# Gather of the first expert right after its one-hot columns, with the expert sorting, one residual scale and the scatter rows placed after it

## Chip, cores and metric

One core of one Trainium2 chip runs the whole program as one launch. The metric is the device time of that core in microseconds (us). Several executions of a kernel are timed and their median is quoted; one more execution is recorded by the hardware profiler, and all rows below come from that one.

## Reference

Two layers run over 256 tokens of 1024 features. Each layer has a mixer with three kinds of attention heads, and then a channel mixer: dense in layer 0, and eight experts of which each token uses its best two in layer 1. Only the expert stage and the step before it matter here:

```python
logits = (t @ w_router).astype(jnp.float32)
top_v, top_i = lax.top_k(logits, TOP_K)
gates = jax.nn.softmax(top_v, axis=-1)
combine = jnp.sum(jax.nn.one_hot(top_i, N_EXPERTS, dtype=jnp.float32) * gates[..., None], axis=1)
for e in range(N_EXPERTS):
    out = out + combine[:, e:e + 1] * swiglu(t, w1[e], w3[e], w2[e])
...
x = layer_norm(DEEPNORM_ALPHA * x + (1.0 + g2) * y, ln2_g[l], ln2_b[l])
```

`swiglu` is `(silu(h @ w1) * (h @ w3)) @ w2` with 1024 x 3584 weights in float32. An expert's three matrices are 44 MB, and all eight are read from HBM.

## Kernel before

The program is one long function, `trunk`, written in the order in which each engine is to run: nothing reorders it. TensorE (PE), VectorE (DVE), ScalarE (ACT) and GpSimd (POOL) each take their own instructions in that order, and the queue SP issues the weight transfers. A transfer waits until the buffer it fills has been read. In the expert stage 16 weight buffers of 1 MB are in turn: five `raws`, three `raws2`, two that were lent by tiles no longer in use, and six made of a `whi` and a `wlo` half (`load_ahead`, L330 and L335).

**Routing** comes after the second layer's mixer. Logits are compared (`choose`), five small matmuls (L1454 to L1458) count who stands before each token, and L1459 writes `slot`, the place of a token in its expert's list. `one_hot(0)` (L1395) turns the first expert's slots into one-hot columns `oh`. Then DVE sorts the experts by how many tokens they have (L1463 to L1494). From that come `slot_at` and `gate_at`, the slots and gates in sorted order, `turn`, the numbers of the experts, which SP reads before it loads the second expert, and `flag`. Expert 0 always comes first and needs no sorting.

**The second residual scale** `grow[1, 1]` has two halves of 512 columns. Each is a bias addition on DVE (`held`, L579), a matmul that spreads a row over all partitions (`later`, L596), and an activation on ACT (L597). The second half is made after the sorting. From the finished scale six ACT copies make the `gain` tiles (L1515).

**Expert stage.** Places with 96 and with 64 columns of tokens alternate; place 0 has 96. For each place:

- `gather(e)` puts four steps in a list. `part(0)` and `part(1)` multiply the normalised tokens `xhat` by `oh` (16 fp32 matmuls of 96 columns in all, L1526), and each scales its half of `xe`, on ACT or, for the second half of place 0, on DVE (`affine`, L619 and L621). `back(0)` and `back(1)` make one-hot rows for the way back: DVE compares (L1534), PE turns (L1538), ACT copies to `ohT` (L1540). `tick()` runs one step of the list.
- Work goes by chunks c = 0 to 3 of the hidden width, here written place/chunk. `up` takes two weight blocks at a time, a group g, in four groups: eight matmuls for the first 64 columns (L1565) into two banks `h`, and eight for the other 32 (L1573) into two banks `hov` that are shared by all chunks and set to 0 once (L1509). After each group it calls `between`, and that calls `tick()`.
- `gated` applies Silu: ACT (L1584) and DVE (L1585) for `h`, then for each `hov` bank an ACT copy (L1591), a DVE addition (L1592) after which the bank is free, Silu on ACT (L1594) and a product on DVE (L1595). It is turned (L1604, in the next chunk's first `between`) and multiplied by `w2` (`down`, L1619 and L1625) after the next chunk's `up`.
- `scatter` multiplies the result by `gain`, adds it to the residual through `ohT`, again as steps.

Place 0 runs its four steps at once, with `tick(4)`, before its first `up`.

Of the kernel before, what the change touches and what calls it, by code (L numbers as in the profile page):

```python
# [9 lines left out]
FT = mybir.dt.float32  # L10
FR = mybir.dt.float32r
BF = mybir.dt.bfloat16
I32 = mybir.dt.int32
AF = mybir.ActivationFunctionType
OP = mybir.AluOpType
AX = mybir.AxisListType.X

S = 256
D = 1024
NB = S // 128  # L20
KD = D // 128
# [103 lines left out]
CAP, BASE = 96, 64  # L125
CAPS = (CAP, BASE) * (NE // 2)
# [4 lines left out]
def trunk(ctx: ExitStack, tc: tile.TileContext, a, out, manual=True):  # L131
    nc = tc.nc
    mm, tr = nc.tensor.matmul, nc.tensor.transpose
    vec, act, pool = nc.vector, nc.scalar, nc.gpsimd
# [3 lines left out]
    small = ctx.enter_context(tc.tile_pool(name="small", bufs=2))  # L138
# [4 lines left out]
    def bank():  # L143
        return psum.tile([128, 512], FT, name="bk", tag="bk")
# [6 lines left out]
    grow = {}  # L151
# [56 lines left out]
    for l in range(2):  # L208
# [28 lines left out]
        if l == 0:  # L237
            ada_weights(0, 11, 12)
            for t in range(12):
# [5 lines left out]
                if t in DENSE_ADA:  # L245
                    n = DENSE_ADA[t]
                    ada_weights(1, n, n + 1)
            ada_weights(1, 5, 6)
        else:
            ada_weights(1, 10, 12)  # L250
            for n in range(NE * 4 + 1):
                e, c = divmod(n, 4)
                if e < NE:
                    k = 8 * 256 // COLS[c]
# [4 lines left out]
                if n > 0:  # L259
                    e, c = divmod(n - 1, 4)  # L260
# [17 lines left out]
    def lend(tag):  # L278

        lent.add(tag)  # L280
        spare.append(tag)
# [109 lines left out]
    start = ExitStack()  # L391
# [33 lines left out]
    ident = cf[:, C_ID:C_ID + 128]  # L425
# [14 lines left out]
    ps = bank()  # L440
# [11 lines left out]
    ps = bank()  # L452
# [6 lines left out]
    ps = bank()  # L459
# [5 lines left out]
    steps = []  # L465
# [3 lines left out]
    def tick(n=1):  # L469
        if sums:  # L470
            sums.pop(0)()
        if aside:
            aside.pop(0)()
        while n > 0 and steps:
            step = steps.pop(0)
            n -= 1
            if step is not None:
                step()
# [18 lines left out]
    later = []  # L497
# [56 lines left out]
    held = []  # L554
# [60 lines left out]
    def affine(f, ps, k0, ac, bc, eng):  # L615
        for i in range(4):
            k = k0 + i
            if eng is act:
                act.activation(f[:, i], ps[:, i], AF.Identity, scale=ac[:, k:k + 1], bias=bc[:, k:k + 1])  # L619
            else:  # L620
                eng.tensor_scalar(f[:, i], ps[:, i], ac[:, k:k + 1], bc[:, k:k + 1], op0=OP.mult, op1=OP.add)  # L621
# [614 lines left out]
    ac = base.tile([128, 8], FT, name="acol", tag="acol", bufs=2)  # L1236
# [43 lines left out]
    for bits in (6, 8, 10, None):  # L1280
        if bits is None:
            c = float(np.float32(rest))
        else:
            e = 2.0 ** (bits - 1 - np.floor(np.log2(rest)))
# [81 lines left out]
    es = ExitStack()  # L1366
    moe = places = None
# [12 lines left out]
    oh, ohT = {}, {}  # L1380
# [6 lines left out]
    slot_at = moe.tile([128, NB, NE], FT)  # L1387
# [3 lines left out]
    def one_hot(e):  # L1391
        n = CAPS[e]
        oh[e] = moe.tile([128, NB, CAP], FT, name="oh", bufs=2)
        for b in range(NB):
            vec.tensor_scalar(oh[e][:, b, 0:n], iota[:, 0:n], (slot if e == 0 else slot_at)[:, b, e:e + 1], None,  # L1395
                              op0=OP.is_equal)

    with tc.tile_pool(name="route", bufs=1) as rt:
        lg = rt.tile([128, NB, NE], FT)
        sel = rt.tile([128, NB, NE], FT)  # L1400
# [27 lines left out]
        def choose(b):  # L1428
# [24 lines left out]
        ps = bank()  # L1453
# [5 lines left out]
        vec.scalar_tensor_tensor(slot, ps[:, 0:16].rearrange("p (b e) -> p b e", b=2), 1.0, sel,  # L1459
                                 op0=OP.add, op1=OP.mult)  # L1460
        one_hot(0)
        num = rt.tile([128, NE], FT)
        vec.tensor_copy(num, ps[:, 16:24])  # L1463
        rank = ranks(num)
# [28 lines left out]
        vec.tensor_scalar(most, most, 0.0, None, op0=OP.max)  # L1493
        vec.tensor_copy(flag, most)  # L1494

    held.pop(0)()
    later.pop(0)()
    gr2 = grow[1, 1]

    with es:
        ep = es.enter_context(tc.tile_pool(name="expert", bufs=1))

        hov = [bank() for _ in range(2)]
        yov = bank()
        for ps in (*hov, yov):
            vec.memset(ps, 0.0)  # L1509

        gain = [ep.tile([128, 512], FT, name=f"gain{i}") for i in range(2)]
        for g, n in zip(gain, (64, 32)):
            for q in range(0, 128, n):
                hf = q // n % 2
                act.activation(g[q:q + n], gr2[q:q + n, 512 * hf:512 * hf + 512], AF.Copy)  # L1515

        def gather(e):
            xe = ep.tile([128, KD, CAP], FT, name="xe", bufs=2)
            n = CAPS[e]

            def part(g):
                ps = bank()[:, 0:4 * n].rearrange("p (k t) -> p k t", k=4)
                for i in range(4):
                    k = 4 * g + i
                    for b in range(NB):
                        mm(ps[:, i], xhat[:, b, 128 * k:128 * k + 128], oh[e][:, b, 0:n], start=b == 0, stop=b == NB - 1)  # L1526
                affine(xe[:, 4 * g:4 * g + 4, 0:n], ps, 4 * g, ac, bc, vec if e == 0 and g == 1 else act)

            def back(v):

                f = small.tile([128, 4, 128], FT, name="aff")
                ps = bank()
                for b in range(NB):
                    vec.tensor_scalar(f[:, 2 * b:2 * b + 2], places[:, 2 * v:2 * v + 2], slot_at[:, b, e:e + 1], None,  # L1534
                                      op0=OP.is_equal)
                for b in range(NB):
                    for hf in range(2):
                        tr(ps[:, 256 * hf + 128 * b:256 * hf + 128 * b + 128], f[:, 2 * b + hf], ident)  # L1538
                ohT[e, v] = moe.tile([128, 2, S], FR, name="ohT", bufs=4)
                act.activation(ohT[e, v], ps.rearrange("p (h t) -> p h t", h=2), AF.Copy)  # L1540

            steps.extend([lambda: part(0), lambda: part(1), lambda: back(0)])
            if n > BASE:
                steps.append(lambda: back(1))
            return xe

        def used_up(raw):
            raw["left"] = 1
# [49 lines left out]
        def gated_turn(e, f, n):  # L1598
            gT = ep.tile([128, 8, CAP], FT, name="egT")
            t = CAPS[e]  # L1600
            for g in range(n // 4):
                ps = bank()
                for j in range(4):
                    tr(ps[:, t * j:t * j + t], f[0:t, 512 * g + 128 * j:512 * g + 128 * j + 128], ident[0:t, 0:t])  # L1604
                ps = ps[:, 0:4 * t].rearrange("p (j t) -> p j t", j=4)
                if g == 0:
                    act.activation(gT[:, 0:4, 0:t], ps, AF.Copy)  # L1607
                else:
                    vec.tensor_copy(gT[:, 4:8, 0:t], ps)  # L1609
            return gT  # L1610
# [70 lines left out]

        work = base.tile([128, 4, 4, 128], FR, name="work", tag="t2")
        order = [(e, c) for e in range(NE) for c in range(4)]
        xes = {0: gather(0)}
        tick(4)
        ys = {}
        fs = {}
        rows = None
# [1 line left out]
        for n in range(len(order) + 1):  # L1690
            if n < len(order):
                e, c = order[n]

                def between(g):

                    if n > 0 and g == 0:
                        fs[n - 1] = gated_turn(order[n - 1][0], fs[n - 1], COLS[order[n - 1][1]] // 128)
                    tick()

                h = up(e, c, xes[e], between)  # L1700
                fs[n] = gated(e, h)
                if e + 1 < NE:
                    if c == 0:
                        one_hot(e + 1)
                    if c == GATHER_AT:
                        xes[e + 1] = gather(e + 1)
                    if (e, c) == ROWS_AT:
                        returned("t3")
                        mid = spread_rows(1, 0)
                        steps.append(lambda: (residual(mid, xhat), aside.append(lambda: lend("t3"))))  # L1710
                    if (e, c) == LEND_TO:
                        lent.clear()
                        spare.clear()
                    if (e, c) == LAST_ROWS_AT:
                        returned("t3")
                        rows = spread_rows(1, 1)
            else:
                fs[n - 1] = gated_turn(NE - 1, fs[n - 1], 4)
            if n > 0:
                pe, pc = order[n - 1]  # L1720
                if pc == 0:
                    ys[pe] = bank()
                if n == len(order):
                    tick(20)
                down(pe, pc, fs.pop(n - 1), ys[pe])
                if pc == 3:
                    scatter(pe, ys.pop(pe))
# [5 lines left out]
    def more(first):  # L1733

        with tc.tile_pool(name="more", bufs=1) as xp:
            en = xp.tile([128, 1], FT)
            vec.memset(en, 1.0)
            with tc.For_i(0, NE, 1) as e:
# [16 lines left out]
                ps = bank()  # L1755
# [4 lines left out]
                for g in range(2):  # L1760
                    ps = bank().rearrange("p (k t) -> p k t", k=4)
                    for i in range(4):
                        k = 4 * g + i
# [3 lines left out]
                y2 = xp.tile([128, D], FT)  # L1767
                for c in range(14):
# [14 lines left out]
                    f = xp.tile([128, 256], FT, name="xg")  # L1783
                    act.activation(f, h1, AF.Silu)
                    vec.tensor_mul(f, f, h3)
                    ps = bank()
# [4 lines left out]
                    for hf in range(2):  # L1791
                        sl = slice(512 * hf, 512 * hf + 512)
                        ps = bank()
# [3 lines left out]
                            vec.tensor_copy(y2[:, sl], ps)  # L1797
                        else:
                            vec.tensor_add(y2[:, sl], y2[:, sl], ps)
                vec.tensor_mul(y2, y2, gr2)  # L1800
                for b in range(NB):
                    for hf in range(2):
                        sl = slice(512 * hf, 512 * hf + 512)
                        ps = bank()
                        mm(ps, o2T[:, 128 * b:128 * b + 128], y2[:, sl], start=True, stop=True)
                        vec.scalar_tensor_tensor(xres[:, b, sl], ps, ge[:, b:b + 1], xres[:, b, sl],
                                                 op0=OP.mult, op1=OP.add)
# [37 lines left out]
```

## Time and profile before

| | us |
|---|---|
| median of 3 runs (lowest, highest) | 1474.82 (1467.89, 1478.98) |
| profiled execution, device time | 1466.8 |
| span of its core in the profile | 1465.0 |

In the profiled execution PE is busy for 1385.7 us, DVE 596.4, ACT 375.9 and POOL 190.6. The device time is 1.8 us more than the span. The stretch around the change lies 570 us after the start of the span. Busy matmul time includes overlap of one matmul with the next, so the chain of waits is the better view for lengths: it says which instruction, one after the other, set the time.

### The profile page before, as it was taken

How to read it: one execution, taken by the hardware profiler on the slowest of the kernel's cores; microseconds unless marked ns; L12 is line 12 of the kernel's file. 1: busy time of each engine (PE TensorE's matmuls, PEld its weight loads, DVE VectorE, ACT ScalarE, POOL GpSimd, SP SyncE). 2: the span in 40 equal slices, each digit the busy share in tenths (PEclk: the TensorE clock that was granted, in tenths of full speed). 3: DMA queues.
4: the chain of work that ended last, by engine and by line, in shares of the span. 5: the costliest groups of instructions: out<-in, count | busy, mean ns of one | idle time of the engine just before them, and what ended most of it. 6: DMA issues, size and time to landing. Idle time of an engine off the chain costs nothing.

```text
span 1465.0 us, 20621 instructions
## 1 busy us (share of the span) xinstructions
PE 1385.7 (95%) x8017; PEld 726.7 (50%) x8017; DVE 596.4 (41%) x1063; ACT 375.9 (26%) x705; POOL 190.6 (13%) x146
## 2 busy tenths in 40 slices
PE   7999899899889897999999999999999999999994
PEld 5876688899778675223233223333223342232331
DVE  3658689999877986111120121110221110320113
ACT  2455354333345543112101112011211110211100
POOL 0202344333244320000300000000000000000000
PEclk9999899999999998999999999999999999999998
DMA  9794587688656339898999999999999999999994
GB/s 320 265 339 175 196 304 257 212 284 282 220 177 217 106 132 363 315 366 325 388 404 407 409 403 407 409 403 409 408 402 409 408 402 409 409 402 408 407 402 157
DMA packets 175497, 480.47 MB, mean 328 GB/s; under 512 B 10848, under 2 KB 44184, under 8 KB 175392
## 3 DMA queue, kind: packets, MB, share of 16 engines
q1 hardware_dynamic: 173820, 475.03, 85.7%
q10 hardware_dynamic: 1572, 4.04, 0.8%
q8 instruction: 65, 1.06, 0.3%
q14 instruction: 40, 0.33, 0.1%
HBM read 477.99 MB, written 1.05 MB: 327 GB/s over the span
## 4 chain that ended last, share of the span: by engine, by line
PE 72%; DVE 15%; issue 6%; DMA 4%; ACT 2%; POOL 1%; SPq 0%; DVEq 0%; ACTq 0%; POOLq 0%
PE bk L1565 26%; PE bk L1619 12%; PE bk L1573 7%; DVE wlo L377 6%; PE bk L1625 4%; PE bk L1085 3%; PE bk L1526 2%; PE bk L1190 2%; PE bk L1644 2%; DVE part L529 2%; DMA rawwlo<-in_w_moe 2%; PE bk L1604 1%; PE bk L740 1%; PE bk L742 1%; PE bk L741 1%
## 5 line engine op out<-in xcount | busy, mean ns | idle before, releaser
L1565 PE MATMUL bk<-raw,xe 128*64 128x512 f32 x1072 | 286.1, 597 | 3.2 <-DMA raw<-in_w_moe 3.2
L377 DVE TENSOR_TENSOR wlo<-raw,whi 128x1024 fp32r<-128x1024 f32 (+3 forms) x146 | 192.1, 1352 | 35.2 <-ACT whi L374 35.1
L1585 DVE TENSOR_TENSOR eg<-aff,bk 64x512 f32<-64x512 f32 x56 | 38.1, 680 | 392.6 <-ACT aff L1584 390.7
L1565 PEld LDWEIGHTS bk<-raw,xe 128*64 128x64 f32 x1072 | 84.0, 136 | 131.1 <-issue 118.9
L374 ACT ACTIVATE whi<-raw 128x1024 fp32r<-128x1024 f32 (+3 forms) x146 | 134.6, 975 | 14.4 <-DVE raw L373 6.0
L1619 PE MATMUL bk<-raw,egT 128*64 128x512 f32 x568 | 134.4, 600 | 0.0
L301 POOL TENSOR_TENSOR raw<-raw,grow 128x1024 f32<-128x1024 f32 x36 | 97.1, 2721 | 138.3 <-DMA raw<-in_w_dense 57.8
L1565 PE MATMUL bk<-rawwhi,xe 128*64 128x512 f32 x360 | 109.5, 601 | 1.8 <-DMA rawwhi<-in_w_moe 1.8
L1565 PE MATMUL bk<-rawwlo,xe 128*64 128x512 f32 x360 | 107.4, 592 | 0.0
L685 POOL TENSOR_TENSOR part<-vrows,cf 78x512 f32<-78x512 f32 x8 | 8.5, 1062 | 752.4 <-DVE eg L1595 723.1
L1584 ACT ACTIVATE aff<-bk 64x512 f32<-64x512 f32 x56 | 33.3, 594 | 284.4 <-PE bk L1565 284.4
L1609 DVE COPY egT<-bk 128x384 f32<-128x384 f32 (+1 forms) x24 | 11.8, 491 | 216.5 <-PE bk L1604 216.5
L1607 ACT ACTIVATE egT<-bk 128x384 f32<-128x384 f32 (+1 forms) x32 | 14.0, 438 | 323.0 <-PE bk L1604 323.0
L1137 PE MATMUL bk<-hT,wlo 128*128 128x256 f32 x320 | 90.8, 284 | 5.1 <-DVE wlo L377 5.0
L1135 PE MATMUL bk<-hT,whi 128*128 128x256 f32 x320 | 90.9, 284 | 0.4 <-ACT whi L374 0.4
L1136 PE MATMUL bk<-hT,whi 128*128 128x256 f32 x320 | 90.7, 283 | 0.0
L740 PE MATMUL bk<-whi,hT 128*128 128x384 f32 (+2 forms) x208 | 78.8, 379 | 2.2 <-ACT hT L1258 1.1
L1619 PEld LDWEIGHTS bk<-raw,egT 128*64 128x64 f32 x568 | 36.7, 136 | 78.7 <-issue 66.0
L741 PE MATMUL bk<-wlo,hT 128*128 128x384 f32 (+2 forms) x208 | 73.8, 355 | 2.0 <-DVE wlo L377 2.0
L1573 PE MATMUL bk<-raw,xe 128*32 128x512 f32 x536 | 74.9, 598 | 0.0
L742 PE MATMUL bk<-whi,hT 128*128 128x384 f32 (+2 forms) x208 | 73.7, 354 | 0.1
L1137 PEld LDWEIGHTS bk<-hT,wlo 128*128 128x128 f32 x320 | 61.1, 191 | 5.9 <-DVE wlo L377 5.9
(324 smaller groups left out, 2124.0 us busy)
## 6 DMA issues: line engine op xcount, KB each, us to landing
raw<-in_w_moe SPq DMA_DIRECT2D x205, 1024.0 KB, 14.2
rawwhi<-in_w_moe SPq DMA_DIRECT2D x131, 512.0 KB, 11.4
rawwlo<-in_w_moe SPq DMA_DIRECT2D x131, 512.0 KB, 11.4
raw<-in_w_ada SPq DMA_DIRECT2D x48, 1024.0 KB, 5.4
raw<-in_w_dense SPq DMA_DIRECT2D x33, 1024.0 KB, 10.1
raw<-in_w_in SPq DMA_DIRECT2D x16, 768.0 KB, 9.2
raw<-in_w_in SPq DMA_DIRECT2D x8, 1024.0 KB, 7.8
raw<-in_w_out SPq DMA_DIRECT2D x8, 1024.0 KB, 5.1
```

The costliest lines, as they stand in the source:

```text
L301: pool.tensor_mul(raw["sb"][:, k], raw["sb"][:, k], grow[raw["gain"]])
L374: act.activation(hi, src, AF.Copy)
L377: eng.tensor_sub(lo, src, hi.bitcast(FT))
L740: mm(pss[b][:, :w], hT[0][:, k, sl], wh[:, i % 2], start=k == 0, stop=False)
L741: mm(pss[b][:, :w], hT[0][:, k, sl], wl[:, i % 2], start=False, stop=False)
L742: mm(pss[b][:, :w], hT[1][:, k, sl], wh[:, i % 2], start=False, stop=k == KD - 1)
L1135: mm(o, w[0][:, k], hT[0][:, k], start=k == 0, stop=False)
L1136: mm(o, w[0][:, k], hT[1][:, k], start=False, stop=False)
L1137: mm(o, w[1][:, k], hT[0][:, k], start=False, stop=k == KD - 1)
L1565: mm(h[hf][q:q + 64], xe[:, k, 0:BASE], at(w, i)[:, sl], start=k == 0, stop=k == KD - 1)
L1573: mm(hov[hf][q:q + 32], xe[:, k, BASE:CAP], at(w, i)[:, sl], start=k < 2, stop=k >= KD - 2)
L1619: mm(y[64 * hf:64 * hf + 64], gT[:, j, 0:BASE], at(w, i)[:, 512 * hf:512 * hf + 512], start=c == 0 and j == 0, stop=c == 3 and j == n - 1)
```

## The change

The first gather is issued directly after `one_hot(0)`, inside the routing, together with the zeroing of the `hov` and `yov` banks and the bias addition of the second scale. Only then comes the sorting. The matmul that spreads the scale, the `gain` copies and the two `back` steps of place 0 become steps of the list, one after each group of the first `up`. Later places keep their order. The compared and the computed values are the same.

```diff
+    def gather(e):
...
+        steps.extend([lambda: part(0), lambda: part(1)])
+        return xe
+
+    def back(e, v):
...
         one_hot(0)
+        assert not steps
+        xes = {0: gather(0)}
+        tick(2)
+
+        hov = [bank() for _ in range(2)]
+        yov = bank()
+        for t in (*hov, yov):
+            vec.memset(t, 0.0)
+        held.pop(0)()
         num = rt.tile([128, NE], FT)
         vec.tensor_copy(num, ps[:, 16:24])
         rank = ranks(num)
...
-    held.pop(0)()
-    later.pop(0)()
-    gr2 = grow[1, 1]
...
+        def gains():
+            for g, n in zip(gain, (64, 32)):
+                for q in range(0, 128, n):
+                    hf = q // n % 2
+                    act.activation(g[q:q + n], grow[1, 1][q:q + n, 512 * hf:512 * hf + 512], AF.Copy)
+
+        steps.extend([later.pop(0), gains, lambda: back(0, 0), lambda: back(0, 1)])
...
-        xes = {0: gather(0)}
-        tick(4)
...
                     if c == GATHER_AT:
                         xes[e + 1] = gather(e + 1)
+                        steps.extend(lambda e=e, v=v: back(e + 1, v) for v in range(2 if CAPS[e + 1] > BASE else 1))
```

Lines of the changed kernel in what follows: gather L1409 (was L1526), turning of the rows L1424 (L1538), `ohT` L1426 (L1540), `gain` L1548 (L1515), exponential of the gates L1507 (L1468), `up` L1570 and L1578 (L1565, L1573), Silu L1589 (L1584).

On PE, from the last counting matmul to the start of chunk 0/1, this stood before:

```order
L1458 MATMUL bk<-selb,cb 128x8
L596 MATMUL bk<-part,ones 128x512
L1526 MATMUL bk<-oh,xhat 128x96 x16
L1538 MATMUL bk<-cf,aff 128x128 x8
L1565 MATMUL bk<-raw,xe 64x512 x8
L1573 MATMUL bk<-raw,xe 32x512 x8
L1565 MATMUL bk<-raw,xe 64x512 x8
```

and this stands there now, to the first matmuls of chunk 0/1 (`rawwhi`):

```order
L1488 MATMUL bk<-selb,cb 128x8
L1409 MATMUL bk<-oh,xhat 128x96 x16
L1570 MATMUL bk<-raw,xe 64x512 x8
L1578 MATMUL bk<-raw,xe 32x512 x8
L596 MATMUL bk<-part,ones 128x512
L1570 MATMUL bk<-raw,xe 64x512 x8
L1578 MATMUL bk<-raw,xe 32x512 x8
L1570 MATMUL bk<-raw,xe 64x512 x8
L1578 MATMUL bk<-raw,xe 32x512 x8
L1424 MATMUL bk<-cf,aff 128x128 x4
L1570 MATMUL bk<-raw,xe 64x512 x8
L1578 MATMUL bk<-raw,xe 32x512 x8
L1424 MATMUL bk<-cf,aff 128x128 x4
L1570 MATMUL bk<-rawwhi,xe 64x512 x4
```

The gather has passed the scale's matmul, which now stands after the first group; the two turnings stand after the third group and after the fourth, the last of chunk 0/0.

On ACT this stood from the exponential of the gates (`lg`) to the first Silu:

```order
L1468 ACTIVATE lg<-lg 128x16
L597 ACTIVATE grow<-bk,alpha 128x512
L1515 ACTIVATE gain_5713<-grow 64x512 x2
L1515 ACTIVATE gain_5714<-grow 32x512 x4
L619 ACTIVATE xe<-bk,bcol,acol 128x96 x4
L1540 ACTIVATE ohT<-bk 128x512 x2
L1584 ACT_TABLE_LOAD
L1584 ACTIVATE aff<-bk 64x512 x2
```

and this stands there now:

```order
L619 ACTIVATE xe<-bk,bcol,acol 128x96 x4
L1507 ACT_TABLE_LOAD
L1507 ACTIVATE lg<-lg 128x16
L597 ACTIVATE grow<-bk,alpha 128x512
L1548 ACTIVATE gain_5737<-grow 64x512 x2
L1548 ACTIVATE gain_5738<-grow 32x512 x4
L1426 ACTIVATE ohT<-bk 128x512 x2
L1589 ACT_TABLE_LOAD
L1589 ACTIVATE aff<-bk 64x512 x2
```

The scaling of `xe` has moved ahead of the exponential. The two `ohT` copies still stand in front of the table load and the first Silu, and each now reads a turning that PE does late in chunk 0/0. On DVE the scaling of the second half of `xe`, the zeroing and the bias addition now stand between `oh` and the first instruction of the sorting. SP's order is the same.

## Rows read from the trace of the kernel before

**Rows 1.** Chain of waits, 530 to 640: start us, length us, engine, tile, line
```profile
567.48 0.96 PE bk L596 x2
...
570.15 0.45 DVE oh L1395 x2
570.60 0.09 DVE num L1463
...
577.87 0.70 DVE part L579
578.57 0.14 issue
578.70 2.05 PE bk L596 x2
580.75 4.53 PE bk L1526 x32
585.30 1.23 DVE xe L621 x4
...
588.09 3.58 PE bk L1565 x16
...
609.84 3.58 PE bk L1565 x16
...
615.28 0.81 PE bk L1604 x8
```
**Rows 2.** Waits of PE, 588 to 1465: total us, times, longest us
```profile
PE bk L1565 <- DMA raw<-in_w_moe: 3.2, 3, 1.7
```
**Rows 3.** Busy us per stretch: PE, PEld, DVE, ACT, POOL, PE clock, DMA share, GB/s
```profile
690.00:716.00 26.00, 26.00 (x133) 6.80 (x128) 2.04 (x3) 3.50 (x6) 4.58 (x4) 1.00 0.97 366
...
590.00:716.00 126.00, 126.00 (x734) 37.23 (x730) 17.79 (x28) 19.09 (x37) 6.75 (x6) 1.00 0.91 339
...
716.00:1436.00 720.00, 714.32 (x3851) 235.80 (x3850) 116.20 (x192) 98.50 (x192) 11.84 (x10) 1.00 1.03 406
```
**Rows 4.** Waits of the DMA queue SP, 590 to 716: total us, times, longest us
```profile
SPq L335 <- PE bk L1573: 51.5, 9, 13.4
```
**Rows 5.** Chain of waits, 765 to 800: gather and turning at place 2
```profile
773.11 1.96 PE bk L1526 x16
...
780.75 0.59 PE bk L1538 x4
```
**Rows 6.** Timeline of ACT: start us, us, what, [idle before and until what]
```profile
526.72 1.28 ACT L1070 ACT_TABLE_LOAD   x1
528.01 0.63 ACT L1070 ACTIVATE rvg<-rvg 128x512 f32<-128x512 f32 x1
...
629.80 0.59 ACT L1584 ACTIVATE aff<-bk 64x512 f32<-64x512 f32 x1 [13.51 <-PE bk L1565]
...
631.61 0.59 ACT L1591 ACTIVATE part<-bk 64x512 f32<-64x512 f32 x1 [0.42 <-PE bk L1573]
...
775.10 1.40 ACT L619 ACTIVATE xe<-bk,bcol,acol 128x96 f32<-128x96 f32 x4 [3.04 <-PE bk L1526]
...
781.38 0.60 ACT L1540 ACTIVATE ohT<-bk 128x512 fp32r<-128x512 f32 x1 [1.05 <-PE bk L1538]
```
**Rows 7.** Timeline of DVE, 578 to 635
```profile
578.66 1.56 DVE L1509 MEMSET bk<- 128x512 f32 x3
...
632.24 0.68 DVE L1592 TENSOR_TENSOR part<-part,bk 64x512 f32<-64x512 f32 x1 [0.34 <-ACT part L1591]
...
634.33 0.68 DVE L1592 TENSOR_TENSOR part<-part,bk 64x512 f32<-64x512 f32 x1
```
**Rows 8.** Stretches of 2 us around the idle time of PE; columns of rows 3
```profile
570.00:572.00 2.00, 0.00 (x0) 0.00 (x0) 1.73 (x11) 0.47 (x1) 0.00 (x0) 1.00 1.01 406
572.00:574.00 2.00, 0.00 (x0) 0.00 (x0) 1.51 (x11) 0.22 (x1) 0.00 (x0) 0.60 1.03 414
...
582.00:584.00 2.00, 2.00 (x17) 2.00 (x16) 0.00 (x0) 1.97 (x4) 0.00 (x0) 0.84 1.02 406
```

More of the change, by code (lines that the diff above doesn't have):

```diff
@@ L1396, in one_hot, with part @@
                               op0=OP.is_equal)
+    ep = es.enter_context(tc.tile_pool(name="expert", bufs=1))
+    def gather(e):
+        xe = ep.tile([128, KD, CAP], FT, name="xe", bufs=2)
+        n = CAPS[e]
+        def part(g):
+            ps = bank()[:, 0:4 * n].rearrange("p (k t) -> p k t", k=4)
+            for i in range(4):
+                k = 4 * g + i
+                for b in range(NB):
+                    mm(ps[:, i], xhat[:, b, 128 * k:128 * k + 128], oh[e][:, b, 0:n], start=b == 0, stop=b == NB - 1)
+            affine(xe[:, 4 * g:4 * g + 4, 0:n], ps, 4 * g, ac, bc, vec if e == 0 and g == 1 else act)
+        steps.extend([lambda: part(0), lambda: part(1)])
+        return xe
+    def back(e, v):
+        f = small.tile([128, 4, 128], FT, name="aff")
+        ps = bank()
+        for b in range(NB):
+            vec.tensor_scalar(f[:, 2 * b:2 * b + 2], places[:, 2 * v:2 * v + 2], slot_at[:, b, e:e + 1], None,
+                              op0=OP.is_equal)
+        for b in range(NB):
+            for hf in range(2):
+                tr(ps[:, 256 * hf + 128 * b:256 * hf + 128 * b + 128], f[:, 2 * b + hf], ident)
+        ohT[e, v] = moe.tile([128, 2, S], FR, name="ohT", bufs=4)
+        act.activation(ohT[e, v], ps.rearrange("p (h t) -> p h t", h=2), AF.Copy)
     with tc.tile_pool(name="route", bufs=1) as rt:
@@ L1494, in trunk @@
         vec.tensor_copy(flag, most)
-    held.pop(0)()
-    later.pop(0)()
-    gr2 = grow[1, 1]
+    assert not held and len(later) == 1
     with es:
[L1504 to L1509, printed above, removed]
-        gain = [ep.tile([128, 512], FT, name=f"gain{i}") for i in range(2)]
[L1512 to L1545, printed above, removed]
@@ L1799, in more @@
                             vec.tensor_add(y2[:, sl], y2[:, sl], ps)
-                vec.tensor_mul(y2, y2, gr2)
+                vec.tensor_mul(y2, y2, grow[1, 1])
                 for b in range(NB):
```

## Prediction

> **What bounds the kernel now.** I read the chain of waits around the change first, because it tells which work sets the time there. At 570.60 `oh` is finished, and the gather needs nothing else that is new. Yet PE starts it at 580.75: in between, the chain runs on DVE through the sorting (570.60 to 577.87), then through the bias addition and the scale's matmul. The first `up` matmul starts at 588.09, chunk 0/1 at 609.84 [rows 1].
>
> Next I asked whether an earlier PE is worth anything, since the expert stage also streams 352 MB of weights. The stretches answer that. From 716 to 1436 the DMA engines move 406 GB/s without a break, while PE is almost always busy but waits for a block here and there (3.2 us for whole `raw` blocks) [rows 2, 3]. So from 716 on the stream sets the end. From 590 to 716 it runs at only 339 GB/s [rows 3]. At 406 the same bytes would take 126 x 339 / 406 = 105.2 us, so 20.8 us of that stretch are holes. The waits of SP tell who made them: it waits for PE, 51.5 us in nine waits on L1573 alone and once 13.4 us, until PE has read a buffer [rows 4]. In this stretch PE leads and the stream follows; 690 to 716 still has holes (366 GB/s) [rows 3]. Whatever PE gains before 716 is therefore passed to the stream, and through it to the end, up to 20.8 us.
>
> **The change part by part.** All times are on the clock of the profiled span; moved work is given its new time.
>
> *Gather.* It can start 0.14 after `oh`, the pause that the chain shows between a DVE result and PE's start: 570.74 [rows 1]. Before, it took 4.53 us after an idle PE, with the clock partly at half. At full clock a half of it takes 1.96 (place 2), so both take 3.92 and end at 574.66 [rows 5]. PE's pause shrinks from 9 us to under 1, so I take full clock. ACT scales the first half in 1.40 [rows 6], from about 572.7 to 574.2, beside the second half of the gather. So `up` starts at 574.66 instead of 588.09.
>
> *What DVE now does before the sorting.* Scaling (1.23), three zeroings (1.56) and bias (0.70) [rows 1, 7] run from 574.7 to about 578.2. `up` reads the second half of `xe` only in its third group, near 586.5. The first L1578 stands 3.58 after the start of `up`, at 578.24, and both `hov` banks are zero by about 577.0. The scale's matmul comes after the first group (5.44 long: chunk 0/0 takes 609.84 - 588.09 = 21.75 [rows 1], a quarter each), at 580.1, when the bias is done. All of this is hidden, with 1.2 us to spare at the nearest place.
>
> *Sorting.* 577.87 - 570.60 = 7.27 us [rows 1], now from 578.2 to 585.5, and the four comparisons of `back` after it (about 1.1) to 586.6. PE wants their result after the third group, near 591.9. It is hidden with 5.3 us to spare. Behind the waiting scaling on DVE only this stands; SP needs `turn` much later.
>
> *Steps put into chunk 0/0.* The scale's matmul at full clock (0.96 [rows 1]) and two turnings of 0.59 [rows 5]. The chunk's groups end at 574.66 + 21.75 + 0.96 + 0.59 = 597.96, and chunk 0/1 starts after the second turning at 598.55. That is 11.29 earlier than 609.84.
>
> *A new wait.* The second `ohT` copy now needs a turning that PE does only at 597.96, and the table load and the first Silu are queued behind it on ACT. Before, Silu of chunk 0/0 began while PE was still in the chunk. Now: the copy begins 0.63 after the turning (781.38 against 780.75) and takes 0.60 [rows 5, 6], to 599.19; the load takes 1.28; with 0.02 of pauses Silu starts at 600.49. From a first Silu to the end of the additions that free the two `hov` banks, chunk 0/1 shows 632.92 - 629.80 and 635.01 - 629.80; without the 0.42 us for which ACT waited there for PE this is 2.70 and 4.79 [rows 6, 7]. So the banks are free at 603.19 and 605.28. PE reaches the first at 598.55 + 3.58 = 602.13 and waits 1.06; its half of L1578 takes 0.93 (half of 615.28 - 609.84 - 3.58), to 604.12, and it waits 1.16 for the second. The turning of chunk 0/0's result then starts at 605.28 + 0.93 = 606.21 instead of 615.28 [rows 1]: 9.07 are left. Bounds: 11.29 if the wait is absent; 7.8 if another step as long as the load lies in that chain. I take 9.1, since each of its pieces has a row.
>
> *The table load.* The trace has one with no other wait around it: loaded from 526.72 for 1.28, next activation at 528.01 [rows 6]. So I count 1.28 and nothing behind it. The Trainium skill (ScalarE: Activation LUTs, section "What ACT_TABLE_LOAD costs") adds a drain of about 1.38 us to each load when the set is switched. By that rule the wait on PE would be 3.60 us and 7.69 us would be left. The trace disagrees: 0.01 us lie behind this load, no 1.38.
>
> *Sum.* The bytes, the buffers and the later chunks are the same, no DMA changes its place on its queue and POOL has no part in this, so every release after 606 comes 9.1 us earlier. This is under the 20.8 us of holes, so all of it reaches the end: 1466.8 - 9.1 = 1457.7 for an execution like the profiled one. The three timed runs and the profiled one have a mean of 1472.1 (1474.82, 1467.89, 1478.98, 1466.8); a median of new runs should lie around that mean less 9.1, at 1463. Against the median of 1474.8 alone it would be 1465.7.
>
> **Rivals**, all from 1472.1.
>
> 1. *The wait for `hov` does not appear*: 11.3 us gained, 1461. It needs the table load or the second copy to run before the turning; the order on ACT speaks against it.
> 2. *The wait is longer*, by a step such as a second 1.28 us: 7.8 gained, 1464.3. This is where the drain would show as well. The load at 526.72 speaks against it.
> 3. *The clock falls all the same.* Before, PE's last work ended at 569.8 and the granted clock was 1.00 until 572, 0.60 from 572 to 574 and 0.84 from 582 to 584, between them 0.50 (1.2 GHz instead of 2.4) [rows 8]. If it fell for those 10.2 us though PE works through them, matmuls would lose half of that, 5.1: gain 3.9, 1468. PE's pause of 0.9 us instead of 9 speaks against it.
> 4. *The stream does not take the gain.* If it, and not PE, set the pace from 590 to 716, the gain is 0: 1472. SP's waits for PE speak against it.
> 5. *Slower.* The sorting now starts 7.6 us later and `slot_at` feeds the turnings inside chunk 0/0, in front of the last quarter of its matmuls. If DVE were held longer, each us beyond the 5.3 to spare stops PE; from 5.3 + 9.1 = 14.4 us on the kernel is slower than before. A delay of 17 us gives 1475. Only the wait of the scaling for the gather is new in front of it, and this is already counted with 4 us, so nothing in the rows makes 14.
> 6. *The gather does not move*: excluded by PE's order.
>
> **How the numbers follow.** Chances: forecast 0.60, rival 1 0.12, rival 2 0.13, rival 3 0.08, rival 4 0.04, rival 5 0.03. A measurement of this kernel can tell about 1%, that is 14.7 us. No case gains that much by itself. But four executions of one kernel lie 12 us apart, so a gain of 8 to 11 us and a draw on the good side, or a median of before on the bad side, may show as over 1%: 0.25 for faster. Slower by over 1% needs rival 5 and a bad draw: 0.03. The rest, 0.72, is within 1%. The cases from 7.8 to 11.3 give 1461 to 1464; with some 8 us of scatter below and above, and rival 3 inside, the range is 1453 to 1473.
>
> **What would show it.** Right: the gather starts near 570.7 and takes about 3.9; no idle time of PE over 1 us before `up`, which starts near 574.7; clock 1.00 throughout; SP's holes between 590 and 716 shrink from 20.8 to under 12 us; PE idle for about 2.2 us in two pieces at L1578 in the first group of chunk 0/1, released by the addition L1597; the stream's last hole about 9 us earlier. Wrong: a clock of 0.50 near 575 to 582, a wait of the first `up` for `xe` or of L1424 for its comparisons, or a last hole that stays at 716.

## The result and the profile after

| | before | changed |
|---|---|---|
| median of 15 runs (lowest, highest), us | 1470.22 (1464.27, 1478.98) | 1461.65 (1456.36, 1466.25) |
| profiled execution, device time | 1466.8 | 1462.73 |
| span | 1465.0 | 1460.9 |
| start of `slot` in the span | 569.94 | 574.88 |
| from the start of `slot` to the end of the span | 895.06 | 886.02 |

The ratio of the times is 0.9932, with a 95% interval from 0.9917 to 0.9946. That is 10.0 us less (7.9 to 12.2), a gain that can be measured and lies within 1%. The two medians themselves lie 8.6 us apart.

The two spans differ by only 4.1 us. The change begins behind `slot`, and the code in front of it is the same, but the profiled execution of the changed kernel came to `slot` 4.94 us later. So the two traces are compared from `slot` on: 895.06 against 886.02, 9.04 us less. In the timelines of DVE that start is the first number, of before and then of the changed kernel (whose second row, the comparisons behind the sorting, is needed further down):

```profile
569.94 0.17 DVE L1459 SCALAR_TENSOR_TENSOR slot<-bk,sel 128x16 f32<-128x16 f32 x1 [0.67 <-PE bk L1458]
```

```profile
574.88 0.17 DVE L1489 SCALAR_TENSOR_TENSOR slot<-bk,sel 128x16 f32<-128x16 f32 x1 [0.67 <-PE bk L1488]
...
590.16 1.13 DVE L1420 TENSOR_SCALAR aff<-places,slot_at 128x256 f32<-128x256 bf16 x4
```

The chain of waits of the changed kernel, which answers to [rows 1] (start us, length us, engine, tile, line):

```profile
575.10 0.28 DVE oh L1395
575.38 0.04 issue
575.42 3.81 PE bk L1409 x32
579.23 3.58 PE bk L1570 x16
...
602.63 0.60 PE bk L1424 x4
603.23 0.02 issue
603.25 0.60 ACT ohT L1426
603.85 0.02 issue
603.87 1.28 ACT L1589
605.15 0.01 issue
605.16 0.60 ACT aff L1589
...
609.81 1.07 PE bk L1578 x8
610.87 0.86 PE bk L1609 x8
```

The reader is to see two things. The sorting is gone from the chain: behind `oh` comes the gather, behind the gather `up`. And at 603.25 the chain leaves PE for ACT: `ohT`, the load of a table, the first Silu. That is the new wait. PE's waits from 588 on show it as the third row here. Those for whole `raw` blocks are as in [rows 2], and the one for a `rawwhi` half took 1.8 us before:

```profile
PE bk L1570 <- DMA raw<-in_w_moe: 3.2, 3, 1.6
PE bk L1570 <- DMA rawwhi<-in_w_moe: 2.3, 1, 2.3
PE bk L1578 <- DVE part L1597: 1.9, 2, 1.0
```

The stretches of the changed kernel, with the columns of [rows 3]. The second and the fourth answer to those rows, the first to [rows 8]:

```profile
576.00:578.00 2.00, 2.00 (x20) 2.00 (x20) 0.00 (x0) 0.52 (x2) 0.00 (x0) 1.00 1.01 404
...
590.00:716.00 126.00, 124.06 (x716) 37.31 (x708) 18.88 (x34) 22.07 (x41) 8.03 (x7) 1.00 0.97 369
...
710.00:712.00 2.00, 2.00 (x9) 0.45 (x6) 0.00 (x0) 0.05 (x1) 0.00 (x0) 1.00 0.90 287
...
716.00:1427.00 711.00, 704.91 (x3810) 232.90 (x3810) 115.49 (x191) 97.30 (x190) 10.57 (x9) 1.00 1.03 406
```

The granted clock is 1.00 while the gather runs. From 590 to 716 the stream moves 369 GB/s instead of 339, so the holes are 126 x (1 - 369 / 406) = 11.5 us instead of 20.8. (At the same distance from `slot` as the window of before, from 594.94 to 720.94, it is 369 as well.) The last hole lies at 710 to 712, 136 us after `slot`. In the trace of before it lay here, 145 us after `slot`:

```profile
714.00:716.00 2.00, 2.00 (x8) 0.44 (x4) 0.00 (x0) 0.00 (x0) 0.00 (x0) 1.00 0.83 301
```

SP's waits for PE at that place, 51.5 us in [rows 4], are down to the row below. Others of them grew a little, so that all of SP's waits for PE in the stretch went from 102.0 to 90.9 us:

```profile
SPq L335 <- PE bk L1578: 35.2, 8, 5.6
```

### The profile page after: what moved, and what is told of

It reads as the page before. It is cut to its first block, busy times and chain, and to the rows that moved or that the text cites. A ratio compares the mean times of both kernels' runs of the same rounds, so it can differ in the third digit from the quotient of the medians.

```text
span 1460.9 us, 20619 instructions
## 1 busy us (share of the span) xinstructions
PE 1387.4 (95%) x8017; PEld 729.5 (50%) x8017; DVE 597.4 (41%) x1063; ACT 375.7 (26%) x705; POOL 191.4 (13%) x146
## 3 DMA queue, kind: packets, MB, share of 16 engines
q8 instruction: 65, 1.06, 0.3%
HBM read 477.99 MB, written 1.05 MB: 328 GB/s over the span
## 4 chain that ended last, share of the span: by engine, by line
PE 71%; DVE 16%; issue 6%; DMA 4%; ACT 2%; POOL 1%; SPq 0%; DVEq 0%; ACTq 0%; POOLq 0%
PE bk L1570 26%; PE bk L1624 12%; PE bk L1578 7%; DVE wlo L377 7%; PE bk L1630 4%; PE bk L1085 3%; PE bk L1409 2%; PE bk L1649 2%; DVE part L529 2%; PE bk L1190 2%; DMA rawwlo<-in_w_moe 2%; PE bk L1609 1%; PE bk L561 1%; ACT whi L374 1%; DMA raw<-in_w_moe 1%
## 5 line engine op out<-in xcount | busy, mean ns | idle before, releaser
L1570 PE MATMUL bk<-raw,xe 128*64 128x512 f32 x1072 | 286.2, 597 | 3.2 <-DMA raw<-in_w_moe 3.2
L377 DVE TENSOR_TENSOR wlo<-raw,whi 128x1024 fp32r<-128x1024 f32 (+3 forms) x146 | 198.3, 1394 | 38.7 <-ACT whi L374 38.6
L1570 PEld LDWEIGHTS bk<-raw,xe 128*64 128x64 f32 x1072 | 84.0, 136 | 130.2 <-issue 118.0
L1570 PE MATMUL bk<-rawwhi,xe 128*64 128x512 f32 x360 | 109.5, 601 | 2.3 <-DMA rawwhi<-in_w_moe 2.3
L1570 PE MATMUL bk<-rawwlo,xe 128*64 128x512 f32 x360 | 107.3, 592 | 0.0
L1589 ACT ACTIVATE aff<-bk 64x512 f32<-64x512 f32 x56 | 33.2, 594 | 267.1 <-PE bk L1570 267.1
L1578 PE MATMUL bk<-raw,xe 128*32 128x512 f32 x536 | 75.0, 598 | 0.0
## 6 DMA issues: line engine op xcount, KB each, us to landing
raw<-in_w_moe SPq DMA_DIRECT2D x205, 1024.0 KB, 14.5
rawwhi<-in_w_moe SPq DMA_DIRECT2D x131, 512.0 KB, 11.5
```

Source lines behind the costliest of these rows:

```text
L377: eng.tensor_sub(lo, src, hi.bitcast(FT))
L1570: mm(h[hf][q:q + 64], xe[:, k, 0:BASE], at(w, i)[:, sl], start=k == 0, stop=k == KD - 1)
L1578: mm(hov[hf][q:q + 32], xe[:, k, BASE:CAP], at(w, i)[:, sl], start=k < 2, stop=k >= KD - 2)
```

## The experiments

All of them are measured in the same way: the time from the start of `slot` to the end of the span in their own profile. Where rounds were run, a ratio with its interval to the kernel before, timed on the same chip, stands beside it. The version with fewer matmuls and the three with zeroings rest on one execution each.

| kernel | `slot` at | span | from `slot` to the end |
|---|---|---|---|
| before, three profiles | 569.94, 568.12, 573.98 | 1465.0, 1464.0, 1471.5 | 895.06, 895.88, 897.52 |
| changed, two profiles | 574.88, 567.89 | 1460.9, 1453.4 | 886.02, 885.51 |
| gather alone in front | 569.11 | 1466.1 | 896.99 |
| sorting first, steps late | 574.44 | 1462.3 | 887.86 |
| both turnings in one step | 574.57 | 1458.4 | 883.83 |
| turnings in place 1 | 573.36 | 1455.6 | 882.24 |
| turnings and scale in place 1 | 574.74 | 1456.4 | 881.66 |
| fewer matmuls | 574.66 | 1451.9 | 877.24 |
| 16, 20, 32 zeroings more on DVE | 575.52, 576.06, 578.09 | 1463.2, 1463.7, 1472.3 | 887.68, 887.64, 894.21 |

### Which half of the change is it?

*Gather alone in front.* DVE's order is that of the change, but the steps run on PE before the first `up`:

```diff
-        steps.extend([later.pop(0), gains, lambda: back(0, 0), lambda: back(0, 1)])
+        later.pop(0)()
+        gains()
+        back(0, 0)
+        back(0, 1)
```

> Edit: the gather, the zeroing and the bias stand where the change puts them, but the scale's matmul, the gain copies and both turnings run before the first `up`, as before. My theory (the head start is only kept if nothing that needs the sorting stands before `up` on PE): `up` starts about 17.0 us after `slot` instead of 18.15 before, and PE idles twice before it, so the clock falls again: 893.9 from `slot` to the end at full clock, up to 899 with 10 us of half clock; no gain that can be told from none. Rival (the earlier gather is itself the gain): 886 to 888.

Measured: 896.99, and a ratio of 0.9983 (0.9963 to 1.0004). PE's timeline, with the idle time before each row in brackets (lines from L1548 on lie 3 further down here):

```profile
569.65 3.81 PE L1409 MATMUL bk<-oh,xhat 128*128 128x96 f32 x32 [0.59 <-DVE oh L1395]
577.27 1.97 PE L596 MATMUL bk<-part,ones 128*128 128x512 f32 x2 [3.81 <-DVE part L579]
584.88 1.94 PE L1424 MATMUL bk<-cf,aff 128*128 128x128 f32 x8 [5.64 <-DVE aff L1420]
586.76 5.74 PE L1573 MATMUL bk<-raw,xe 128*64 128x512 f32 x16
```

The gather is early, and nothing comes of it: PE then waits 3.81 us for the bias and 5.64 for the sorting, and `up` starts 17.7 us after `slot`, almost as late as before (18.15). The granted clock is 0.50 from 578 to 590, so the first group takes 5.74 us instead of 3.65. A matmul that is early is worth nothing as long as the next one on PE's list waits for the same result.

*Sorting first, steps late.* The other half: PE's order is that of the change, while on DVE the scaling, the zeroing and the bias addition stand behind the sorting. The block from `xes = {0: gather(0)}` to `held.pop(0)()` moves:

```diff
         one_hot(0)
-        xes = {0: gather(0)}
...
         vec.tensor_copy(flag, most)
+        xes = {0: gather(0)}
```

> Edit: the sorting stands before the scaling of the second half of `xe`, the zeroing and the bias on DVE, as before the change; PE's order is that of the changed kernel (gather directly behind the counting matmuls, scale and turnings inside chunk 0/0). My theory (what counts is that PE's gather no longer stands behind a matmul that waits for the sorting): gather and first `up` start as in the changed kernel; `hov` is zero 1.5 us too late and the bias 0.7 us too late for PE, so 888.1 from `slot` to the end, 7.0 less than before. Rival (the place on DVE directly behind `oh` is what counts): about 894, nearly all lost.

Measured: 887.86, and 0.994 (0.9918 to 0.9962). PE's timeline has one new wait:

```profile
578.72 3.65 PE L1570 MATMUL bk<-raw,xe 128*64 128x512 f32 x16
584.12 1.92 PE L1578 MATMUL bk<-raw,xe 128*32 128x512 f32 x16 [1.75 <-DVE bk L1532]
```

`up` starts 4.28 us after `slot`, as in the timeline of the changed kernel (579.16 - 574.88), and L1578 waits 1.75 us for the zeroed banks. So most of the gain, 7.2 of 9.0 us, comes from the new order on PE, the early gather together with the late steps. The new order on DVE adds the rest, 1.8, once PE's order is there; without the late steps it adds nothing.

### Is the wait at L1578 what was said of it?

*Both turnings in one step*, after the third group, so that the second `ohT` copy is over long before Silu:

```diff
-        steps.extend([later.pop(0), gains, lambda: back(0, 0), lambda: back(0, 1)])
+        steps.extend([later.pop(0), gains, lambda: (back(0, 0), back(0, 1))])
```

> Measure in the profile: from the start of `slot` to the end of the span; before 895.06 us (1465.0 - 569.94), changed kernel 886.02 (1460.9 - 574.88). Edit: both turnings of place 0 stand after the third group, so that both `ohT` copies and the table load are done before Silu is wanted. My theory (the new wait of PE at L1578 costs 2.2 us, and the stream hands on all of it): that wait is gone, 883.8 from `slot` to the end, 11.3 less than before. Rival (the stream has already taken all it can, or the wait is covered later): 886.0, the wait gone but no gain.

*Turnings in place 1.* Both become steps of the first `up` of place 1, where the stream is nearly in the lead:

```diff
+                    if (e, c) == (0, 3):
+                        steps.extend(lambda v=v: back(0, v) for v in range(2))
```

> Edit: the turnings and `ohT` copies of place 0 move out of chunk 0/0 to the list of steps after chunk 0/3, where the stream and not PE sets the time. My theory: the wait at L1578 goes (2.2 us) and two turnings of 0.59 leave the stretch in which PE leads: 3.4 us less than the changed kernel, 882.6 from `slot` to the end. Rival (the stretch in which PE leads is over earlier, so only the wait counts): 883.8. Rival (the stream takes no more): 886.0.

Measured: 883.83 with 0.9903 (0.988 to 0.9926), and 882.24 with 0.9894 (0.9871 to 0.9917). PE's timelines of the first and of the second have no wait in chunk 0/1:

```profile
596.22 1.09 PE L1424 MATMUL bk<-cf,aff 128*128 128x128 f32 x8
...
608.12 0.88 PE L1609 MATMUL bk<-cf,eg 96*128 96x96 f32 x8
```

```profile
598.60 1.92 PE L1578 MATMUL bk<-raw,xe 128*32 128x512 f32 x16
...
605.89 0.88 PE L1609 MATMUL bk<-cf,eg 96*128 96x96 f32 x8
```

The chunk's result is turned 33.55 and 32.53 us after `slot`, in the changed kernel 35.92 (610.80 - 574.88). So the wait goes when the copy no longer stands behind PE's last step, and with it 2.4 us at this place and 2.2 at the end. Moving the turnings out of the stretch gives another 1.6. Their own length is 1.2 of that; the other 0.4 is no more than two profiles of one kernel differ by (0.5 us for the changed kernel, see below).

*Turnings and scale in place 1.* The scale's matmul and the `gain` copies follow them:

```diff
-        steps.extend([later.pop(0), gains])
...
                     if (e, c) == (0, 3):
+                        steps.extend([later.pop(0), gains])
                         steps.extend(lambda v=v: back(0, v) for v in range(2))
```

> The spreading of the second scale, the `gain` copies and both turnings of place 0 become steps of the first `up` of place 1, where the stream is about to lead. With two turnings only moved this way, 882.24 us lay between `slot` and the end. If PE's steps before the last hole of the stream (about 134 us after `slot` there) each cost their own length, the scale's matmul (1.06) goes as well: 881.2. Rival: the hole that is left there belongs to the stream's own order and the scale's matmul was no longer worth anything: 882.2. A second rival: the ACT copies, now in front of a Silu, or the late `ohT` hold PE up in place 1: over 883.

Measured: 881.66, between the two expectations, and 0.9888 (0.987 to 0.9907), a median of 1458.35 us. Of the matmul's 1.06 us about 0.6 came through, and since that is near the 0.5 us between two profiles of one kernel, it isn't shown that the move was worth anything. PE's new wait in place 1 is short (0.87 us before the first turning at 727.22, 20 us behind the last hole) and cannot be seen at the end. By the timed runs this version and the one before it are alike. Both beat the changed kernel by about 4 us from `slot` on.

### Does the stream take all that PE gains?

*Fewer matmuls.* The second set of `up` matmuls is left out in three chunks, to give PE a far larger lead:

```diff
-                for j in range(0, ks if CAPS[e] > BASE else 0, 2):
+                for j in range(0, ks if CAPS[e] > BASE and (e > 0 or c > 2) else 0, 2):
```

> This kernel leaves out the matmuls for the last 32 token columns (L1578) in chunks 0, 1 and 2 of place 0, so its output lacks those products. That takes 3 x 4 x 1.86 = 22.3 us of PE's work out of the stretch in which PE leads. My theory (a gain of PE is handed on only up to the holes of the stream, 20.8 us before and 9.0 of them used): 11 to 12 us less than the changed kernel, 874 to 875 from `slot` to the end, and no holes left. Rival (PE leads throughout): 863.7. Rival (the stream took all it can already): 886.

Measured: 877.24. The stretch has no hole left:

```profile
590.00:716.00 126.00, 122.16 (x636) 39.22 (x634) 24.08 (x42) 25.13 (x46) 14.35 (x12) 0.99 1.03 407
```

PE's last matmul on weights and the sending of the output by SP, of this kernel and then of before:

```profile
1428.65 1.08 PE L1624 MATMUL bk<-rawwlo,egT 128*64 128x512 f32 x4 [0.18 <-DMA rawwlo<-in_w_moe]
...
1441.83 2.32 SPq L1685 DMA_DIRECT2D out<-out  x4
```

```profile
1443.88 1.08 PE L1619 MATMUL bk<-rawwlo,egT 128*64 128x512 f32 x4 [0.17 <-DMA rawwlo<-in_w_moe]
...
1457.07 2.32 SPq L1680 DMA_DIRECT2D out<-out  x4
```

The last matmul on weights ends 1429.73 - 574.66 = 855.07 us after `slot`, in before 1444.96 - 569.94 = 875.02. These 19.95 us stand against the 20.8 us of holes, so the limit was there, and the changed kernel used less than half of it (8.90 at this place). Against the changed kernel 11.05 us are gained here, as expected.

At the end of the span only 17.8 us are left, and the difference lies in the very last part. In both kernels SP begins to send the output 12.1 us after the last matmul on weights. From there to the end of the span it is 10.1 us instead of 7.9. The queue SP shows 5.0 us of waiting for its own instructions there, in two pieces, and 2.8 in one piece before. The last instruction of DVE ends 8.1 us before the end of the span, and 5.7 to 6.0 in the 13 other profiles. Why the end was longer in this one execution stays open. The granted clock isn't the reason: it is lower at the last seven matmuls (0.70 from 1432 to 1434), which take 2.63 us instead of 1.90, but they took 3.06 in the version with turnings and scale in place 1, and its end was as short as the others. The expectation had left this tail as it was, and so missed by 2.2 to 3.2 us.

### How much time has the sorting to spare?

*32, 16 and 20 zeroings more* on DVE, between the bias addition and the sorting (a tile that nothing reads):

```diff
         held.pop(0)()
+        fill = rt.tile([128, 256], FT)
+        for _ in range(32):
+            vec.memset(fill, 0.0)
```

> Edit: 32 fillings of a scratch tile (about 8.5 us in all) on DVE in front of the sorting. The changed kernel's trace has the first two comparisons of the turnings done at 590.7 and PE asking for them at 596.5, so 5.9 us to spare. My theory: the first turning waits for the filling's length less 5.9, about 2.6 us, and 888.6 from `slot` to the end. Rival (the sorting is still on the path in full): 894.5. Rival (also this is hidden): 886.0.

> 16 zeroings of a 128x256 tile on DVE between the bias addition and the sorting, of which 32 took 12.41 us before, so 6.21 us of delay. From the run with 32, where PE waited 6.32 us, the comparisons have 12.41 - 6.32 = 6.09 us to spare: a wait of about 0.1 us at the first L1424 and 886.0 to 886.3 from `slot` to the end, as without the zeroings (886.02). Rival (to spare 5.3, as predicted): a wait of 0.9 and 886.9. If any delay of the sorting counted in full, 892.2.

> 20 of the same zeroings, 7.76 us. To spare 6.09: a wait of 1.67 us at the first L1424, the granted clock stays at 1.00, and 887.7 from `slot` to the end. Rival (to spare 5.3): a wait of 2.5 and 888.5. If the clock falls after so short a wait too, as it did after 6.32 us: some 1.5 more, 889.2.

Measured: 894.21, 887.68 and 887.64. With 32, DVE's and PE's timelines say:

```profile
586.21 12.41 DVE L1503 MEMSET fill<- 128x256 f32 x32
```

```profile
606.12 1.11 PE L1424 MATMUL bk<-cf,aff 128*128 128x128 f32 x4 [6.32 <-DVE aff L1420]
607.17 4.70 PE L1573 MATMUL bk<-raw,xe 128*64 128x512 f32 x16
```

The zeroings took 12.41 us, not the 8.5 that I had reckoned with. PE waited 6.32, so 6.1 were to spare, close to the 5.9 of the expectation. In the wait the granted clock also fell (0.62 from 602 to 604, 0.50 from there to 608), and the turning and the next group took 0.5 and 1.05 us more: 7.9 in all, and 8.2 more at the end. That the result lies near the number of the rival theory is an accident of the wrong length.

With 20, which take 7.71 us, PE waits 1.63 us: again 6.1 to spare, and 887.64 where 887.7 was expected. The clock stays at 1.00 here.

```profile
599.40 0.70 PE L1424 MATMUL bk<-cf,aff 128*128 128x128 f32 x4 [1.63 <-DVE aff L1420]
```

With 16 (6.15 us) PE waits less than 0.1 us at this place, as expected, and yet 1.7 us are lost. PE's timeline and the stretches show where:

```profile
608.53 0.62 PE L1581 MATMUL bk<-rawwhi,xe 128*32 128x512 f32 x2 [0.92 <-DVE part L1600]
...
610.61 1.00 PE L1581 MATMUL bk<-rawwhi,xe 128*32 128x512 f32 x2 [1.02 <-DVE part L1600]
...
612.42 1.54 PE L1612 MATMUL bk<-cf,eg 96*128 96x96 f32 x8
```

```profile
610.00:612.00 2.00, 1.39 (x8) 0.16 (x8) 1.27 (x3) 0.63 (x1) 0.00 (x0) 0.68 1.01 403
612.00:614.00 2.00, 2.00 (x14) 1.36 (x12) 0.39 (x2) 0.49 (x1) 0.00 (x0) 0.50 1.04 414
```

The two waits of the changed kernel are unchanged in length, but here the granted clock fell at the second of them. In the five other profiles that have these two waits it stayed at 1.00, as in this stretch of the changed kernel, which holds its second wait:

```profile
608.00:610.00 2.00, 0.98 (x12) 0.16 (x8) 1.36 (x2) 1.14 (x3) 0.00 (x0) 1.00 1.04 416
```

What makes it fall in one and not in the others isn't shown.

### Where does the scatter of the times come from?

Both kernels once more, unchanged:

> The kernel before once more, unchanged, for a second profile of it. If the scatter of its times lies in the work ahead of `slot`, which the change does not touch, `slot` starts at another time than 569.94 us while the length from `slot` to the end stays within 0.5 of 895.06. Rival: the length from `slot` to the end differs by 2 us or more from execution to execution, as it would if the granted clock fell differently in the idle time of PE; then single profiles don't measure the change to a microsecond, and the timed gains that are 2 to 5 us larger than those from `slot` on would come from there.

> The kernel before a third time: as for the second, 895.06 within 0.5 if the scatter lies ahead of `slot`, 897 or more in one of the two if it doesn't.

> The changed kernel once more, unchanged. From `slot` to the end 886.02 within 0.5 if the scatter lies ahead of `slot`. Rival: the two waits at L1578 sometimes bring the granted clock down, as in the run with 16 zeroings, where it cost about 1.6 us: 887.6.

Measured: 895.88, 897.52 and 885.51. The start of `slot` moved by 5.9 us over the three profiles of before, and by 7.0 between the two of the changed kernel. Most of the scatter therefore lies in unchanged code ahead of `slot`. Which instructions make it wasn't searched for. But before also varies behind `slot`, by 2.5 us, and both theories are right in part. The chain of waits of its third profile, and its stretches with the columns of [rows 3]:

```profile
573.98 0.19 DVE slot L1459
...
584.77 5.29 PE bk L1526 x32
...
591.73 1.94 PE bk L1538 x8
593.67 4.31 PE bk L1565 x16
```

```profile
590.00:592.00 2.00, 0.32 (x3) 0.30 (x3) 1.91 (x7) 0.63 (x2) 0.00 (x0) 0.92 1.01 403
592.00:594.00 2.00, 2.00 (x10) 1.56 (x10) 0.37 (x2) 0.89 (x2) 0.00 (x0) 0.50 1.04 416
594.00:596.00 2.00, 2.00 (x8) 0.52 (x6) 0.00 (x0) 1.58 (x2) 0.00 (x0) 0.72 0.57 219
```

The gather that took 4.53 us in [rows 1] takes 5.29 here (in the second profile 4.79): the clock comes back at another moment after PE's idle time, 0.50 from 580 to 588 and 0.93 from 588 to 590. Then it falls a second time. While the second half of `xe` is scaled and compared, PE idles for 1.68 us in front of the turnings. That idle time is there in the first profile too, and the clock stays at 1.00 in it; here it is 0.50 from 592 to 594, and the turnings take 1.94 us instead of 1.15, the first group 4.31 instead of 3.58. Together the clock makes 2.28 of the 2.46 us by which this profile is longer than the first. In the second profile it makes 0.26 of 0.82; where the rest lies wasn't searched for.

So the profile that the prediction rests on was the best of three for before. The mean of before is 896.15, that of the changed kernel 885.77: 10.4 us apart. Against this mean the versions with moved turnings gain 12.3, 13.9 and 14.5 us from `slot` on. Their timed medians lie 14.3, 16.2 and 16.4 us below the kernel before. The difference of some 2 us between the two ways of measuring isn't explained.

## Why the prediction was right

The forecast was the likeliest case and it came: a gain of 9.1 us, 9.04 between the two traces from `slot` on, and 10.0 us (7.9 to 12.2) in the timed runs. The predicted 1463 stands against a median of 1461.65; the mean of 1472.1 that it started from stands against a median of 1470.22 over 15 runs, so 1463 was too high by the starting point and not by the gain.

- *Gather.* Predicted 3.92 us at full clock right behind `oh`; measured 3.81 at 1.00. It starts 0.54 us after `slot` instead of 0.80, because it waits only for the first of the two halves of `oh`. `up` starts 4.35 us after `slot`, predicted 4.72.
- *DVE's work before the sorting.* Hidden, as predicted. The experiment that puts it behind the sorting makes the wait appear, 1.75 us.
- *Sorting.* Predicted 5.3 us to spare. The comparisons end at 591.29 and PE's third group at 596.60, which is 5.3. But the first turning needs only the first of the four (590.16 and a quarter of 1.13, so 590.44), and 6.1 us can be lost before PE stops. With 7.71 us added it waited 1.63.
- *Steps in chunk 0/0.* Predicted 0.96 and twice 0.59; measured 1.06, 0.59 and 0.60.
- *The new wait.* Predicted 1.06 and 1.16 at L1578; measured 0.92 and 1.02. From the first Silu to the two free banks it took 2.51 and 4.60 us, predicted 2.70 and 4.79. The versions without the late copy have no wait there, so the cause is shown.
- *The table load.* Predicted 1.28 us with nothing behind it. In the chain it ends at 605.15 and Silu starts at 605.16. The drain of 1.38 us, which the Trainium skill (ScalarE: Activation LUTs, section "What ACT_TABLE_LOAD costs") adds, does not appear here either; with it the wait would have been 3.3 us instead of 1.9.
- *Sum.* At the turning of chunk 0/0's result 9.35 us are gained (by the chains of waits 45.34 after `slot` before, 35.99 now), predicted 9.07. The pieces are off by a few tenths each and in part cancel: `up` starts 0.37 earlier and the wait is 0.28 shorter than predicted, other steps are longer. At the last weights 8.90 are left and at the end 9.04.
- *The stream.* It took what PE gained, and its limit is the size of the holes: 19.95 us reached, 20.8 estimated.

Of the rivals, the first (no wait, 11.3 us) is what the version with both turnings in one step gives: 895.06 - 883.83 = 11.2. The second and the fourth did not come. The third, a fall of the clock, did not come at the gather; but in the run with 16 zeroings it came at the new wait, and cost 1.7 us. How often this happens in the changed kernel, its two profiles can't tell. The fifth needed a delay of 14.4 us in the sorting; what was measured is near it: 12.41 us more on DVE would leave 2.0 by its sum, and left 0.9 against the first profile of before, since the clock fell too.

One term was sized too small. The gain from the clock was taken from one profiled execution, in which the gather took 4.53 us. Over three profiles that gather, the turnings and the first group take 9.26, 9.52 and 11.54 us, and in neither profile of the changed kernel does the clock fall there. This makes 0.85 of the 1.1 us by which the mean of before lies above its first profile. Between the means of the profiles lie 10.4 us instead of 9.1, and the timed gain of 10.0 agrees with that.

## What to carry to other kernels

In a program that runs in written order, an early result is worth only as much as the instruction that stands next on the waiting engine's list: look at what that one waits for, and move those steps as well. Put short steps that are needed late where another resource (here the weight stream) is in the lead, and not in front of a copy that an activation stands behind. And before two traces are subtracted, anchor both at the last instruction that the change leaves alone: 5 of the 9 us would otherwise have been lost in the scatter ahead of it.

## What was not expected

- The start of `slot`, before which nothing was changed, lay between 567.89 and 578.09 us over the 14 profiles.
- The granted clock came back at different moments after the same idle time of PE, and in one of three profiles of before it fell again in an idle time of 1.68 us. This makes 2.3 us between executions.
- At two waits of 0.92 and 1.02 us the clock fell to 0.50 in one profile and stayed at 1.00 in five.
- 32 zeroings of a 128x256 tile in a row took 12.41 us on DVE, 0.39 us each.
- The end of the program, behind DVE's last instruction, took 8.1 us in one profile and 5.7 to 6.0 in the 13 others.
